# A matmul with bias and residual: the fourth x tile loaded behind W, transposes in the middle of a tile's products, another transfer list

## The chip, the core and the metric

The kernel runs on one core of one Trainium2 chip. The metric is the device time in microseconds (us); smaller is better. The core has five engines that matter here: TensorE (PE in the profile, with its weight loads as PEld), VectorE (DVE), ScalarE (ACT), GpSimd (POOL) and SyncE (SP). SP computes nothing in this kernel. It only issues the transfers between HBM and SBUF. Every transfer is cut over the core's 16 DMA engines, which work in parallel, each in the order of issue.

## The reference

```python
batch, m, k, n = 16, 512, 1024, 768      # all float32
def reference(x, weight, bias, residual):
    return (np.matmul(x, weight) + bias + residual).astype(np.float32)
```

Flattened, x is 8192 x 1024, W is 1024 x 768, and residual and output are 8192 x 768.

## The kernel before, in words

The 8192 rows are worked through as 64 tiles (t = 0 to 63) of 128 rows each, in four groups S of 16 tiles (J = 16). Row number (S, p, j) of x lies in partition p of tile 16 S + j, so that a transfer of several neighbouring tiles moves one long piece for each partition.

SBUF holds a ring X of 16 x tiles in float32, a ring R of 32 rows (one row is a 128 x 768 residual tile, which becomes the output tile in place), a ring XB of four casted tiles, a ring XT of four transposed tiles, and W in bf16 (w_sb). PSUM holds three product tiles PO and two transpose tiles PT. W arrives in four chunks q of 256 rows of K each; its staging place is rows 14 to 21 of R, and it is cast from there into w_sb by operations called wc.

Each tile t takes these steps:

- cast(t): ACT turns the float32 tile X into bf16 XB (in the head VectorE takes some or half of them; "sv" means that ACT and VectorE take a half each).
- transp(t): TensorE transposes the tile in four matrix instructions (two bf16 values are moved as one float32 word) into PT, and VectorE copies PT into XT.
- mm(t, q): for one chunk q of W, two weight loads and four matmuls, two 512 and two 256 columns wide. mm_all(t, range(n_q)) takes all n_q = 4 chunks, so sixteen matmuls a tile.
- finish(t): VectorE adds PSUM and the R row. For t below 14 (EARLY_END), residual has not come yet. There finish writes product plus bias into a spare row of R, and GpSimd adds the residual later. From tile 14 on, GpSimd adds bias to the residual row first, and finish(t) needs that row.
- pool_adds: GpSimd goes through the list ADDS, and stops at the first entry whose residual row or finish isn't there yet in program order.

The order of the work is written out by hand. HEAD_ORDER is the order of the first three tiles' products (HEAD = 3), which run chunk by chunk of W across the tiles, with dummy matmuls (warm) where TensorE would idle. The loop from L352 on takes the tiles 3 to 62, one each: cast of t + 2, GpSimd's adds, transposes of t + 1, all products of t, finish of t - 1. Tile 63 closes the kernel in two pieces of 512 and 256 columns (LAST).

ORDER is the list of transfers, and SP issues them in exactly this order (pump, L174). An entry is (kind, S, first j, end j): 'x' and 'r' load tiles of x and residual, 'w' and 'b' load a chunk of W and the bias, 's' stores output rows, 'c' stores a piece of the last tile. If an entry has to wait, all the entries behind it wait too. An x tile waits for the cast of the tile 16 before it (the ring X), a residual row from tile 32 on waits for the landing of the store of the row 32 before it (the ring R), and a store waits for the finishes or adds of its rows. A wait for a transfer is a wait for all 16 of its DMA engines.

```python
    for t in range(HEAD, n_t):
        cast(t + 2)
        pool_adds(t + 1)
        transp(t + 1)
        if t < n_t - 1:
            mm_all(t, range(n_q))
        finish(t - 1)
        pool_adds(t + 1)
```

Of the kernel before, what the change touches and what calls it, by code (L numbers as in the profile page):

```python
# [19 lines left out]
EARLY_END = 14  # L20
TMP_ROW = 16
W_ROW = 14
ADDS = [10, 14, 3, 2, 4, 15, 11, 1, 5, 13, 7, 6, 12, 9, 0, 8]
HEAD_ORDER = [('cast', 0, 'v'), ('cast', 1, 's'), ('tr', 0), ('tr', 1), ('wc', 0, 0, 's'), ('wc', 0, 1, 'g'),
 ('warm', 3), ('mm', 0, 0), ('mm', 1, 0), ('cast', 2, 'sv'), ('cast', 3, 'sv'), ('warm', 3),
 ('tr', 2), ('tr', 3), ('wc', 1, 0, 's'), ('wc', 1, 1, 'v'), ('mm', 2, 0), ('mm', 0, 1),
 ('mm', 1, 1), ('mm', 2, 1), ('wc', 2, 0, 's'), ('wc', 2, 1, 'v'), ('mm', 0, 2), ('mm', 1, 2),
 ('mm', 2, 2), ('wc', 3, 0, 's'), ('wc', 3, 1, 'v'), ('bias',), ('cast', 4, 'sv'), ('mm', 0, 3),
 ('fin', 0), ('mm', 1, 3), ('mm', 2, 3)]
ORDER = [('x', 0, 0, 2), ('w', 0, 0, 2), ('x', 0, 2, 4), ('w', 1, 0, 2), ('b', 0, 0, 0), ('w', 2, 0, 2),  # L30
 ('w', 3, 0, 2), ('x', 0, 4, 6), ('x', 0, 6, 10), ('r', 0, 0, 6), ('x', 0, 10, 14),
 ('r', 0, 6, 16), ('x', 0, 14, 16), ('x', 1, 0, 6), ('r', 1, 0, 6), ('x', 1, 6, 16),
 ('r', 1, 6, 16), ('s', 0, 0, 16), ('x', 2, 0, 6), ('r', 2, 0, 6), ('x', 2, 6, 16),
 ('r', 2, 6, 16), ('s', 1, 0, 16), ('x', 3, 0, 6), ('r', 3, 0, 7), ('x', 3, 6, 16),
 ('r', 3, 7, 16), ('s', 2, 0, 16), ('s', 3, 0, 10), ('s', 3, 10, 13),
 ('s', 3, 13, 15), ('c', 3, 15, 0), ('c', 3, 15, 1)]
OUTSIDE = 4
LAST = [(0, 512), (512, 256)]

# [78 lines left out]
def kernel(  # L118
# [14 lines left out]
    n_q = K // (2 * P)  # L133
    n_t = M // P
# [29 lines left out]
    def rows(a, b, cs=range(len(chunks))):  # L164
        return [("R", r % RR, c) for r in range(a, b) for c in cs]
# [4 lines left out]
    done = set()  # L170
    queue = list(ORDER)
    stores = []
# [48 lines left out]
    def mark(*what):  # L221
        done.add(what)
        pump()

    def copy(eng, dst, src, rd, wr):
        op(eng, lambda e: (e.copy if eng == "act" else e.tensor_copy)(out=dst, in_=src), rd, wr)  # L226

    def plus(eng, dst, a, b, rd, wr):
        op(eng, lambda e: e.tensor_add(out=dst, in0=a, in1=b), rd, wr)  # L229
# [4 lines left out]
    def cast(t, how="s"):  # L234
        if t < n_t:
            assert ("x", t) in done, t
            src, dst, h = X[:, t % XR, :], XB[t % XB_N], K // 2
            rd, wr = [("X", t % XR)], [("XB", t % XB_N, i) for i in range(2)]
            if how == "sv":
                copy("act", dst[:, 0:h], src[:, 0:h], rd, wr[:1])  # L240
                copy("dve", dst[:, h:K], src[:, h:K], rd, wr[1:])
            else:
                copy("act" if how == "s" else "dve", dst, src, rd, wr)
            mark("cast", t)

    def transp(t):
        if t < n_t:
            words, pt = XB[t % XB_N].bitcast(FP32), PT[t % 2]
            for q in range(n_q):
                op("pe", lambda e, q=q: e.transpose(out=pt[:, q, :], in_=words[:, ts(q, P)], identity=ident),  # L250
                   [("XB", t % XB_N, 2 * q // n_q), "ident"], [("PT", t % 2)])
            copy("dve", XT[t % XT_N].rearrange("p q m e -> p (q m e)"),
                 pt.rearrange("p q m -> p (q m)").bitcast(BF16), [("PT", t % 2)], [("XT", t % XT_N)])
# [11 lines left out]
    def mm(t, q, e, parts, po, wr):  # L265

        lhsT, rd = XT[t % XT_N][:, q, :, e], [("XT", t % XT_N)]
        op("pe", lambda g: g.ldweights(lhsT), rd)  # L268
        for n0, nl, to in parts:
            times(po[:, to:to + nl], lhsT, w_sb[:, q, e, n0:n0 + nl], q == 0 and e == 0, q == n_q - 1 and e == 1,  # L270
                  [*rd, ("w", q, e)], [wr])

    def mm_all(t, qs):
        for q in qs:
            for e in range(2):
                mm(t, q, e, [(n0, nl, n0) for n0, nl in chunks], PO[t % HEAD], ("PO", t % HEAD))

    def row(t, n0=0, nl=N):
        return R[:, t % RR, n0:n0 + nl]

    def tmp(t):
        return R[:, TMP_ROW + t, :]

    adds = list(ADDS) + list(range(max(ADDS) + 1, n_t))

    def pool_adds(upto):
        for t in [t for t in adds if t <= upto]:
            if ("r", t) not in done or (t < EARLY_END and ("fin", t) not in done):
                return
            adds.remove(t)  # L290
            r, rk = row(t), rows(t, t + 1)
            if t < EARLY_END:
                plus("pool", r, r, tmp(t), rk + rows(TMP_ROW + t, TMP_ROW + t + 1), rk)
                mark("add", t)
                mark("out", t)
            else:
                plus("pool", r, r, bias_sb, rk + ["bias"], rk)
                mark("add", t)

    def finish(t):  # L300
        p, pk = PO[t % HEAD], ("PO", t % HEAD)
        if t < EARLY_END:
            plus("dve", tmp(t), p, bias_sb, [pk, "bias"], rows(TMP_ROW + t, TMP_ROW + t + 1))
            mark("fin", t)
        else:
            assert ("add", t) in done, t
            plus("dve", row(t), p, row(t), [pk] + rows(t, t + 1), rows(t, t + 1))
            mark("out", t)
# [18 lines left out]
    for kind, *a in HEAD_ORDER:  # L327
# [10 lines left out]
        elif kind == "wc":  # L338
            q, e, eng = a
            r = W_ROW + 2 * q + e  # L340
# [11 lines left out]
    for t in range(HEAD, n_t):  # L352
        cast(t + 2)
        pool_adds(t + 1)
        transp(t + 1)
        if t < n_t - 1:
            mm_all(t, range(n_q))
        finish(t - 1)
        pool_adds(t + 1)
    t = n_t - 1  # L360
    for i, (n0, nl) in enumerate(LAST):
        b = (t - 2 * i) % HEAD
# [45 lines left out]
```

## Time and profile before

| what | value |
|---|---|
| time, median of 3 runs (lowest, highest) | 210.14 us (210.11, 210.18) |
| span of the profiled execution, first to last instruction | 208.5 us |
| what the median holds beyond that span | 1.6 us |
| TensorE busy | 201.6 us, 97% |
| the transfer queue's share of 16 DMA engines | 97.9% |
| VectorE, ScalarE, GpSimd busy | 105.3, 66.1 and 115.2 us |
| bytes read, written | 61.88 MB, 25.17 MB |
| transfers in the list | 33 |

For the profiled execution itself, the profile gives the span and no separate device time. The span runs on the profile's own clock from the first to the last instruction; the runs' times were taken without it. So the two are compared through the 1.6 us between span and median. The busy shares of two resources are above 97%, TensorE's and the DMA engines', and a share alone doesn't tell which of the two sets the end. That needs the last few microseconds of the trace.

### The profile page before, as it was taken

How to read it: one execution, taken by the hardware profiler on the slowest of the kernel's cores; microseconds unless marked ns; L12 is line 12 of the kernel's file. 1: busy time of each engine (PE TensorE's matmuls, PEld its weight loads, DVE VectorE, ACT ScalarE, POOL GpSimd, SP SyncE). 2: the span in 40 equal slices, each digit the busy share in tenths (PEclk: the TensorE clock that was granted, in tenths of full speed). 3: DMA queues.
4: the chain of work that ended last, by engine and by line, in shares of the span. 5: the costliest groups of instructions: out<-in, count | busy, mean ns of one | idle time of the engine just before them, and what ended most of it. 6: DMA issues, size and time to landing. Idle time of an engine off the chain costs nothing.

```text
span 208.5 us, 2492 instructions
## 1 busy us (share of the span) xinstructions
PE 201.6 (97%) x1298; PEld 80.8 (39%) x794; DVE 105.3 (51%) x141; ACT 66.1 (32%) x69; POOL 115.2 (55%) x71
## 2 busy tenths in 40 slices
PE   7899999999999999999999999999999999999991
PEld 2333434443443444344334434433443443344340
DVE  1457555445545543654554454555445545544542
ACT  2444522402640282420280094230092047430000
POOL 1100029859999904999029801999207960899200
PEclk9999999999999999999999999999999999999998
DMA  5999999899999999999998999999999999999985
GB/s 216 425 425 445 426 423 475 385 427 425 485 409 416 449 395 438 453 396 437 410 493 387 432 445 429 443 443 385 423 450 468 416 398 471 415 443 417 427 351 232
DMA packets 4627, 87.20 MB, mean 418 GB/s; under 512 B 516, under 2 KB 644, under 8 KB 1416
## 3 DMA queue, kind: packets, MB, share of 16 engines
q1 hardware_dynamic: 4616, 87.05, 97.9%
q8 instruction: 8, 0.13, 0.2%
q14 instruction: 3, 0.02, 0.0%
HBM read 61.88 MB, written 25.17 MB: 417 GB/s over the span
## 4 chain that ended last, share of the span: by engine, by line
PE 92%; DMA 4%; DVE 1%; SPq 0%; ACT 0%; issue 0%
PE psum_o L257 79%; PE pt L250 13%; DMA x_tile<-in_x_dram 4%; SPq L168 0%; DVE xt L226 0%; ACT xb L226 0%; DVE ro L229 0%; SPq L403 0%; SPq L371 0%
## 5 line engine op out<-in xcount | busy, mean ns | idle before, releaser
L257 PE MATMUL psum_o<-w_sb,xt 128*128 128x256 bf16 (+1 forms) x1024 | 176.6, 326 | 0.5 <-DVE xt L226 0.5
L229 POOL TENSOR_TENSOR ro<-ro,bias_sb 128x768 f32<-128x768 f32 x50 | 88.8, 1817 | 46.9 <-DMA ro<-in_residual_dram 46.9
L226 ACT CAST xb<-x_tile 128x1024 bf16<-128x1024 f32 (+1 forms) x63 | 61.3, 1023 | 117.1 <-DMA x_tile<-in_x_dram 88.6
L268 PEld LDWEIGHTS <-xt 128*128 128x128 bf16 x520 | 50.9, 98 | 102.9 <-issue 101.0
L226 DVE COPY xt<-pt 128x1024 bf16<-128x1024 bf16 x64 | 44.1, 691 | 83.4 <-PE pt L250 83.4
L229 DVE TENSOR_TENSOR ro<-psum_o,ro 128x768 f32<-128x768 f32 (+2 forms) x51 | 47.6, 934 | 6.5 <-POOL ro L229 4.5
L250 PE MATMUL pt<-ident,xb 128*128 128x128 f32 x256 | 38.3, 274 | 0.6 <-DVE xb L226 0.4
L229 POOL TENSOR_TENSOR ro<-ro 128x768 f32<-128x768 f32 x14 | 24.9, 1818 | 25.0 <-DMA ro<-in_residual_dram 24.9
L250 PEld LDWEIGHTS pt<-ident,xb 128*128 128x128 f32 x256 | 29.7, 141 | 15.6 <-issue 12.3
L229 DVE TENSOR_TENSOR ro<-psum_o,bias_sb 128x768 f32<-128x768 f32 x14 | 13.2, 948 | 0.0
L312 PE MATMUL psum_o<-warm 128*128 128x512 bf16 x18 | 6.3, 506 | 1.4 <-DVE warm_a L232 1.4
L226 DVE CAST xb<-x_tile 128x512 bf16<-128x512 f32 (+1 forms) x4 | 1.9, 492 | 6.2 <-DMA x_tile<-in_x_dram 6.2
L226 ACT CAST w_sb<-ro 128x768 bf16<-128x768 f32 x4 | 3.3, 832 | 3.7 <-DMA ro<-in_weight_dram 3.7
L226 POOL CAST w_sb<-ro 128x768 bf16<-128x768 f32 x1 | 0.8, 822 | 6.0 <-DMA ro<-in_weight_dram 6.0
L312 PEld LDWEIGHTS psum_o<-warm 128*128 128x128 bf16 x18 | 2.1, 124 | 4.5 <-issue 2.7
L226 DVE CAST w_sb<-ro 128x768 bf16<-128x768 f32 x3 | 1.7, 557 | 2.0 <-DMA ro<-in_weight_dram 2.0
L226 ACT ACT_TABLE_LOAD x1 | 1.3, 1283 | 0.9 <-SPq L371 0.9
L329 DVE STREAM_SHUFFLE bias_sb<-bias_row 128x768 f32<-128x768 f32 x1 | 1.0, 1007 | 0.0
L232 DVE MEMSET warm<- 128x256 uint32 x1 | 0.3, 272 | 1.1 <-SPq L371 1.1
L232 DVE MEMSET bias_row<- 128x768 f32 x1 | 0.7, 698 | 0.2 <-issue 0.2
L232 POOL MEMSET ident<- 128x128 f32 x1 | 0.2, 204 | 0.5 <-SPq L371 0.5
L320 POOL TENSOR_SCALAR_AFFINE_SELECT ident<-ident 128x128 f32<-128x128 f32 x1 | 0.3, 292 | 0.2 <-POOL ident L232 0.2
(7 smaller groups left out, 0.7 us busy)
## 6 DMA issues: line engine op xcount, KB each, us to landing
out_dram<-ro SPq DMA_DIRECT2D x3, 6144.0 KB, 34.6
x_tile<-in_x_dram SPq DMA_DIRECT2D x3, 5120.0 KB, 24.5
ro<-in_residual_dram SPq DMA_DIRECT2D x3, 3840.0 KB, 32.4
x_tile<-in_x_dram SPq DMA_DIRECT2D x3, 3072.0 KB, 34.0
ro<-in_residual_dram SPq DMA_DIRECT2D x3, 2304.0 KB, 18.7
x_tile<-in_x_dram SPq DMA_DIRECT2D x4, 1024.0 KB, 10.9
x_tile<-in_x_dram SPq DMA_DIRECT2D x2, 2048.0 KB, 23.4
out_dram<-ro SPq DMA_DIRECT2D x1, 3840.0 KB, 13.3
```

Source lines behind the costliest of these rows:

```text
L226: op(eng, lambda e: (e.copy if eng == "act" else e.tensor_copy)(out=dst, in_=src), rd, wr)
L229: op(eng, lambda e: e.tensor_add(out=dst, in0=a, in1=b), rd, wr)
L232: op(eng, lambda e: e.memset(dst, v), [], [wr])
L250: op("pe", lambda e, q=q: e.transpose(out=pt[:, q, :], in_=words[:, ts(q, P)], identity=ident), [("XB", t % XB_N, 2 * q // n_q), "ident"], ...
L257: return e.add_instruction(mybir.InstMatmult(name=nc.get_next_instruction_name(), ins=[e.lower_ap(rhs), e.lower_ap(lhsT, for_matmul_weight ...
L268: op("pe", lambda g: g.ldweights(lhsT), rd)
L312: op("pe", lambda e: e.matmul(PO[i][:, 0:512], lhsT=warm[:, 0:P], rhs=warm, start=True, stop=True), ["warm"], [("PO", i)])
L320: op("pool", lambda e: e.affine_select(out=ident, in_=ident, compare_op=mybir.AluOpType.not_equal, fill=1.0, base=0, pattern=[[-1, P]], ch ...
L329: op("dve", lambda e: e.stream_shuffle(out=bias_sb, in_=bias_row, mask=[0] * QUAD), ["bias_row"], ["bias"])
```

## The change

Four things are changed, and nothing that is computed:

- ORDER: x tiles 2 and 3 are two transfers now. Tile 2 stays ahead of the second chunk of W, and tile 3 goes behind the fourth. The x, residual and store entries after that are cut elsewhere, and three of the old pieces are spread out: group 2's residuals are loaded in four pieces, its predecessor's store (group 1) in two pieces between them, and the last four residual rows are loaded behind the store of group 2. The list has 39 entries where it had 33.
- HEAD_ORDER: tile 2 is cast, transposed and multiplied alone, the second run of three dummy matmuls is gone, tile 3 is cast after the last chunk of W and transposed between the last products of tiles 1 and 2, and the bias is spread (bias) earlier. The cast of tile 4 goes to ACT alone, at the head's end.
- The loop: the transposes of tile t + 1 stand between the products of chunks 0, 1 and of chunks 2, 3 of tile t, and finish(t - 1) with GpSimd's adds stands ahead of them.
- ADDS: GpSimd takes the first sixteen rows in their natural order.

```diff
--- before.py
+++ after.py
@@ -20,20 +20,19 @@
 EARLY_END = 14
 TMP_ROW = 16
 W_ROW = 14
-ADDS = [10, 14, 3, 2, 4, 15, 11, 1, 5, 13, 7, 6, 12, 9, 0, 8]
+ADDS = [0, 1, 2, 3, 4, 5, 6, 7, 8, 9, 10, 11, 12, 13, 14, 15]
 HEAD_ORDER = [('cast', 0, 'v'), ('cast', 1, 's'), ('tr', 0), ('tr', 1), ('wc', 0, 0, 's'), ('wc', 0, 1, 'g'),
- ('warm', 3), ('mm', 0, 0), ('mm', 1, 0), ('cast', 2, 'sv'), ('cast', 3, 'sv'), ('warm', 3),
- ('tr', 2), ('tr', 3), ('wc', 1, 0, 's'), ('wc', 1, 1, 'v'), ('mm', 2, 0), ('mm', 0, 1),
- ('mm', 1, 1), ('mm', 2, 1), ('wc', 2, 0, 's'), ('wc', 2, 1, 'v'), ('mm', 0, 2), ('mm', 1, 2),
- ('mm', 2, 2), ('wc', 3, 0, 's'), ('wc', 3, 1, 'v'), ('bias',), ('cast', 4, 'sv'), ('mm', 0, 3),
- ('fin', 0), ('mm', 1, 3), ('mm', 2, 3)]
-ORDER = [('x', 0, 0, 2), ('w', 0, 0, 2), ('x', 0, 2, 4), ('w', 1, 0, 2), ('b', 0, 0, 0), ('w', 2, 0, 2),
- ('w', 3, 0, 2), ('x', 0, 4, 6), ('x', 0, 6, 10), ('r', 0, 0, 6), ('x', 0, 10, 14),
- ('r', 0, 6, 16), ('x', 0, 14, 16), ('x', 1, 0, 6), ('r', 1, 0, 6), ('x', 1, 6, 16),
- ('r', 1, 6, 16), ('s', 0, 0, 16), ('x', 2, 0, 6), ('r', 2, 0, 6), ('x', 2, 6, 16),
- ('r', 2, 6, 16), ('s', 1, 0, 16), ('x', 3, 0, 6), ('r', 3, 0, 7), ('x', 3, 6, 16),
- ('r', 3, 7, 16), ('s', 2, 0, 16), ('s', 3, 0, 10), ('s', 3, 10, 13),
- ('s', 3, 13, 15), ('c', 3, 15, 0), ('c', 3, 15, 1)]
+ ('warm', 3), ('mm', 0, 0), ('mm', 1, 0), ('cast', 2, 'sv'), ('tr', 2), ('mm', 2, 0), ('wc', 1, 0, 's'),
+ ('wc', 1, 1, 'v'), ('mm', 0, 1), ('mm', 1, 1), ('mm', 2, 1), ('bias',), ('wc', 2, 0, 's'),
+ ('wc', 2, 1, 'v'), ('mm', 0, 2), ('mm', 1, 2), ('mm', 2, 2), ('wc', 3, 0, 's'), ('wc', 3, 1, 'v'),
+ ('cast', 3, 'sv'), ('mm', 0, 3), ('fin', 0), ('mm', 1, 3), ('tr', 3), ('mm', 2, 3), ('cast', 4, 's')]
+ORDER = [('x', 0, 0, 2), ('w', 0, 0, 2), ('x', 0, 2, 3), ('w', 1, 0, 2), ('b', 0, 0, 0), ('w', 2, 0, 2),
+ ('w', 3, 0, 2), ('x', 0, 3, 4), ('x', 0, 4, 6), ('x', 0, 6, 9), ('r', 0, 0, 7), ('x', 0, 9, 13),
+ ('r', 0, 7, 16), ('x', 0, 13, 16), ('x', 1, 0, 7), ('r', 1, 0, 7), ('x', 1, 7, 16), ('r', 1, 7, 16),
+ ('s', 0, 0, 16), ('x', 2, 0, 7), ('r', 2, 0, 2), ('r', 2, 2, 9), ('x', 2, 7, 16), ('r', 2, 9, 12),
+ ('s', 1, 0, 8), ('r', 2, 12, 16), ('s', 1, 8, 16), ('x', 3, 0, 6), ('r', 3, 0, 6), ('x', 3, 6, 16),
+ ('r', 3, 6, 12), ('s', 2, 0, 16), ('r', 3, 12, 16), ('s', 3, 0, 4), ('s', 3, 4, 11), ('s', 3, 11, 14),
+ ('s', 3, 14, 15), ('c', 3, 15, 0), ('c', 3, 15, 1)]
 OUTSIDE = 4
 LAST = [(0, 512), (512, 256)]
 
@@ -352,11 +351,13 @@
     for t in range(HEAD, n_t):
         cast(t + 2)
         pool_adds(t + 1)
+        if t < n_t - 1:
+            mm_all(t, range(n_q // 2))
+        finish(t - 1)
+        pool_adds(t + 1)
         transp(t + 1)
         if t < n_t - 1:
-            mm_all(t, range(n_q))
-        finish(t - 1)
-        pool_adds(t + 1)
+            mm_all(t, range(n_q // 2, n_q))
     t = n_t - 1
     for i, (n0, nl) in enumerate(LAST):
         b = (t - 2 * i) % HEAD
```

## Prediction

> **What bounds the kernel now.** I read the page first (shares and slices), then the chain of waits, then the last microseconds. From the page:
>
> ```profile
> PE 201.6 (97%) x1298; PEld 80.8 (39%) x794; DVE 105.3 (51%) x141; ACT 66.1 (32%) x69; POOL 115.2 (55%) x71
> ...
> DMA  5999999899999999999998999999999999999985
> ...
> q1 hardware_dynamic: 4616, 87.05, 97.9%
> ```
>
> Two candidates: TensorE and the transfers are both above 97%. The chain of waits names TensorE:
>
> ```profile
> by line: PE psum_o L257 79.4%; PE pt L250 13.0%; DMA x_tile<-in_x_dram 3.9%; SPq L168 0.4%; DVE xt L226 0.3%; ACT xb L226 0.3%; issue 0.3%; DVE ro L229 0.2%; SPq L403 0.0%; SPq L371 0.0%
> ...
> 12.22 6.74 PE psum_o L257 x40
> 19.00 0.66 PE pt L250 x4
> ...
> 22.38 0.44 PE pt L250 x4
> 22.81 2.60 PE psum_o L257 x16
> ```
>
> From 12.2 us on TensorE has no gap: a tile costs 0.44 for four transposes and 2.60 for sixteen products, 3.04. But this view goes back from the last store to the engine that released it. It doesn't ask whether that store then stood behind others. VectorE's timeline and a table of the last stages do:
>
> ```profile
> 201.65 0.96 DVE L229 TENSOR_TENSOR ro<-psum_o,ro 128x768 f32<-128x768 f32 x1 [1.11 <-PE psum_o L257]
> 203.30 0.69 DVE L229 TENSOR_TENSOR ro<-psum_o,ro 128x512 f32<-128x512 f32 x1 [0.70 <-PE psum_o L257]
> 204.18 0.42 DVE L229 TENSOR_TENSOR ro<-psum_o,ro 128x256 f32<-128x256 f32 x1 [0.18 <-PE psum_o L257]
> ```
>
> ```profile
> 200.00:201.00 1.00, 1.00 (x8) 0.32 (x4) 0.53 (x1) 0.00 (x0) 0.00 (x0) 1.00 0.73 307
> ...
> 202.00:203.00 1.00, 1.00 (x6) 0.49 (x5) 0.60 (x1) 0.00 (x0) 0.00 (x0) 1.00 0.68 286
> 203.00:204.00 1.00, 1.00 (x10) 0.69 (x7) 0.69 (x1) 0.00 (x0) 0.00 (x0) 1.00 0.74 310
> 204.00:205.00 1.00, 0.14 (x2) 0.00 (x0) 0.42 (x1) 0.00 (x0) 0.00 (x0) 1.00 1.03 418
> ```
>
> The last two columns are the DMA engines' share and GB/s. Some engines are idle from 200 to 204, and it looks as if stores were missing. The landing marks of the single DMA engines say otherwise. Rows 48 to 57 land between 199.41 (first engine) and 201.69 (last), rows 58 to 60 between 202.13 and 204.44, rows 61 and 62 between 205.73 and 206.28, the two last pieces at 206.93 and 207.27 at the latest. The last engine took 2.75, 1.84, 0.65 and 0.34 us for its 73.7, 49.2, 16.4 and 8.2 KB, which is 24 to 27 GB/s: it has no gap to the end. Following the last landings backwards I find none at all back to the first transfer (14.52 us for the store of 81.00 to 95.52, 12.14 for the x load of 157.66 to 169.80, 27 GB/s each). So the late DMA engine sets the end, and the fast ones idle for it. TensorE ties with it: released at 202.61, the store of rows 61 and 62 landed on the fast engines only 0.55 us before the late one.
>
> **The head: a gain on TensorE.** An x tile is 32.8 KB an engine. Packets in the trace take 309 ns for 8192 bytes and 1815 for 49152, so 27.2 GB/s and 8 ns for each packet: a tile takes 1.20 us. With tile 3 behind W, chunk 1 lands at 11.96 - 1.20 = 10.76, chunk 2 at 12.70, chunk 3 at 14.57, tile 3 at 15.85, tiles 4 and 5 at 18.3 as before. Tile 2 lands at 8.88; cast 0.62, transposes from 9.8 on (after the products that ended at 9.79), copy 0.69, product of chunk 0 at 11.1, where before it began at 12.22. Then nine (tile, chunk) units of 0.65: chunk 2 is wanted at 13.7 (cast 13.6), chunk 3 at 15.7 (cast 15.4). The second three dummies fall out of a stretch in which TensorE waited anyway. Tile 3 is transposed at 17.0, the first three tiles end near 18.0, tile 3's products at 21.15 with tile 4's transposes in them. Before, the same work was done at 22.21: gain 1.06. Two moved steps cost nothing here: the bias spread (1.01 on VectorE, its row landed by 11.0) fits between the cast of chunk 1 (to 11.7) and chunk 2's landing at 12.70, and would push chunk 2's cast by what it is late; tile 4's cast, 1.04 on ACT alone, ends at 19.3, and its transposes are wanted at 19.4. Bounds: a gain of 0.8 (ACT and VectorE each 0.1 to 0.2 late at one chunk) to 1.1.
>
> **The transposes in mid-tile.** The same instructions, so no busy time. What moves is cover: the copy XT (0.69) of the next tile has 1.30 us of products after the transposes, where it had 2.60. It stands behind finish(t - 1) (0.95) on VectorE, which starts with the tile. So if finish waits for GpSimd over 1.30 + 0.44 + 1.30 - 0.95 - 0.69 = 1.4 us, TensorE stalls.
>
> **x and residual cut elsewhere.** x 6 to 8 lands at 18.25 + 3.69 = 21.94. Residual 0 to 6 (7 rows of 0.90, 6.40 with packets) would follow at 28.34. One engine lost 1.32 us in this place before: residual 0 to 5 landed at 28.14 to 28.64 on 15 engines and at 29.96 on the last, after a 16 KB instruction packet at 23.84. I keep that: 29.66. x 9 to 12 lands at 34.55, cast ends at 35.7:
>
> ```profile
> 30.03 10.67 POOL L229 TENSOR_TENSOR ro<-ro 128x768 f32<-128x768 f32 x6 [21.57 <-DMA ro<-in_residual_dram]
> ...
> 34.93 3.89 ACT L226 CAST xb<-x_tile 128x1024 bf16<-128x1024 f32 x4 [7.81 <-DMA x_tile<-in_x_dram]
> ```
>
> The lower line is where tile 10 came at almost the same time, wanted at 37.4. Now tile 9 comes there, wanted at 22.45 + 4 x 3.04 = 34.6: stall 1.1 us (0.4 if the late engine were only 0.6 late), and the head's gain is spent. The other batches keep a margin after that (tile 32: cast by 105.1, wanted at 105.6).
>
> **ADDS in natural order.** Residual 7 to 15 lands at 42.8; nine adds of 1.78 (six in 10.67) put row 14 seven places back, done at 57.0. Product 14 ends at 55.7. So finish(14) waits 1.3, just under the 1.4 that the copy allows, and row 16 (landed near 61.5, added by 63.3, wanted at 61.8) waits 1.5: 0 to 0.3 us of stall, I take 0.15. TensorE ends 0.2 later than before, net: -1.06 + 1.1 + 0.15.
>
> **Six more transfers.** One more x entry, three more residual, two more stores. Each is eight more packets an engine: 8 x 8 ns, and a semaphore packet of 9 ns: 0.075 us. Landings agree: loads of 65.5 and 327.7 KB an engine take 2.48 and 12.14, of which the bytes explain all but 0.07 to 0.1. The late engine has no gap to hide it in: 6 x 0.076 = 0.46 us. Lower bound by the last small stores (0.04 each): 0.24. No place of the new list lets SP run dry: the longest wait, residual 32 for the landing of group 0's store near 95, has 8.5 us of x behind that store in the queue.
>
> The Trainium skill speaks against small transfers: DMA: Bandwidth & Descriptors, section "Bandwidth", wants 1 MiB and more for each, and its "Anatomy" section gives each a fixed cost of about 2.0 us. By that, six would add 12 us and the time would be about 222; as the landings show 0.07 to 0.1 in a full queue, I take this as latency that a queue hides.
>
> The same skill's TensorE: Matmul & The Clock Gate, Part 1, has the clock halved after an idle window of about 3.4 us. The new stall is 1.1 us, the trace of before shows no idle time of that length after 6.5 us and a mean clock of 0.996, so no run here shows it yet; if the stall did halve the clock for one window, some 1.7 us more would be spent.
>
> **The end.** The last full store is one row instead of two, so TensorE's side lies 1.2 us ahead of the late engine: finish(62) ends near 202.8, transfers began to move some 1.3 us after their release in this place before (202.61, first landing 205.73, less 1.84), and the row's turn in the late queue is near 205.3. So 0.2 us later on TensorE costs nothing, and the transfers' 0.46 all arrives: span 208.5 + 0.46 = 209.0, and with the same 1.6 us around it 210.14 + 0.46 = 210.60. A measurement can tell about 0.2%, 0.42 us, from no change: the forecast is just above it.
>
> **The rivals.**
> - The transfers' fixed cost is half: 210.4, no difference. For it: the small stores at the end. Against: packets and loads. 0.19.
> - Faster: the lateness of the last engine (2.3 us behind the first) comes from instruction packets, and another list may shift which engine they hit. If it shrinks by over 0.9 us, the saving beats the 0.46; TensorE's side then stops it at 0.7 below the time before: 209.4 to 209.7. Against: the packets come about every 24 us with TensorE's program, which keeps its length. 0.09.
> - Slower by more: TensorE binds, as the stall at tile 9 and GpSimd's waits add up to twice what I found, against 1.06 gained. TensorE's side lies 1.2 ahead of the late engine's new end, and 0.2 of the net loss is in that already; so the point is a net loss of 1.4 (stalls of 2.5), and beyond it each 0.1 is paid: with stalls of 3.0, 210.60 + 0.5 = 211.1. Rows 14 and 16 lie near the edge. 0.12.
> - The forecast, 210.4 to 210.8: 0.60, two thirds of it above the 0.2%.
>
> Slower 0.40 + 0.12 = 0.52, same 0.20 + 0.19 = 0.39, faster 0.09. The range 210.1 to 211.2 leaves out the faster rival and the far end of the slower one.
>
> **What would show it.** Right: TensorE's products of tile 0 to 2 end near 18.0; one wait of the transposes for ACT of about 1.1 near 34.6; GpSimd waits on VectorE of 1.3 and 1.5 near 57 and 63; last landings 0.3 to 0.5 later than 207.27, and the last engine without a gap. Wrong: a stretch where SP waits and the DMA share falls below 0.9 in mid-span; a late engine that is not 2 us late; TensorE's last product after 205; a clock below 0.99.

## The result, and the profile after

The changed kernel takes 210.72 us (median of 8 runs, 210.66 to 210.83), beside 210.16 us for the kernel before (8 runs, 209.92 to 210.39). The ratio is 1.0026 with a 95% interval of 1.0016 to 1.0037, so it is slower by 0.56 us, or 0.26%. The span of the profiled execution goes from 208.5 to 208.9 us; the profiled run itself took 210.69 us.

The page of the changed kernel, the lines that answer to those of before:

```profile
PE 200.0 (96%) x1270; PEld 81.0 (39%) x791; DVE 110.2 (53%) x140; ACT 67.1 (32%) x69; POOL 115.4 (55%) x71
...
q1 hardware_dynamic: 5480, 87.05, 97.9%
```

The queue moves the same 87.05 MB in 5480 packets instead of 4616. Those are six more transfers of 8 payload packets and a semaphore packet on each of the 16 engines: 6 x 16 x 9 = 864. Its share is still 97.9%, so the longer list filled more time and not less. The chain of waits names TensorE in 79% of the span (67.6 and 11.6) and a load of x in 13.5%:

```profile
by line: PE psum_o L256 67.6%; DMA x_tile<-in_x_dram 13.5%; PE pt L249 11.6%; SPq L167 2.5%; issue 1.2%; DVE ro L228 0.9%; ACT xb L225 0.5%; DVE xt L225 0.3%; SPq L404 0.0%; DVEq L103 0.0%; ACTq L103 0.0%; SPq L372 0.0%
```

TensorE's timeline shows where that load comes in, and a second place where TensorE stands. The bracket at the end is the idle time ahead of the group, and its releaser. It counts from the modelled end of the group before; sixteen products follow each other in 2.60 us, and by that the two places cost 1.14 us (34.78 to 35.92) and 0.48 us (58.97 to 59.45):

```profile
32.17 2.76 PE L256 MATMUL psum_o<-w_sb,xt 128*128 128x512 bf16 x16
35.92 0.66 PE L249 MATMUL pt<-ident,xb 128*128 128x128 f32 x4 [0.99 <-ACT xb L225]
...
57.67 1.46 PE L256 MATMUL psum_o<-w_sb,xt 128*128 128x512 bf16 x8
59.45 1.48 PE L256 MATMUL psum_o<-w_sb,xt 128*128 128x512 bf16 x8 [0.31 <-DVE xt L225]
```

The first is tile 9: its x landed at 34.75. The second is the copy XT of tile 16, late behind finish(14). VectorE's timeline has that, the head, and the end:

```profile
16.44 0.96 DVE L228 TENSOR_TENSOR ro<-psum_o,bias_sb 128x768 f32<-128x768 f32 x1 [0.17 <-PE psum_o L256]
17.53 0.69 DVE L225 COPY xt<-pt 128x1024 bf16<-128x1024 bf16 x1
...
57.84 0.96 DVE L228 TENSOR_TENSOR ro<-psum_o,ro 128x768 f32<-128x768 f32 x1 [2.31 <-PE pt L249]
58.71 0.68 DVE L225 COPY xt<-pt 128x1024 bf16<-128x1024 bf16 x1
...
63.60 0.96 DVE L228 TENSOR_TENSOR ro<-psum_o,ro 128x768 f32<-128x768 f32 x1 [1.51 <-POOL ro L228]
...
204.55 1.02 DVE L228 TENSOR_TENSOR ro<-psum_o,ro 128x512 f32<-128x512 f32 x2 [1.21 <-PE psum_o L256]
```

The last piece is added by 205.57, where before it was 204.60. The table of the last stages (the columns are as before: granted clock, the five engines, clock, DMA share, GB/s):

```profile
204.00:205.00 1.00, 0.95 (x9) 0.60 (x7) 0.45 (x1) 0.00 (x0) 0.00 (x0) 1.00 0.89 356
205.00:206.00 1.00, 0.00 (x0) 0.00 (x0) 0.57 (x2) 0.00 (x0) 0.00 (x0) 1.00 0.39 156
206.00:207.00 1.00, 0.00 (x0) 0.00 (x0) 0.00 (x0) 0.00 (x0) 0.00 (x0) 1.00 0.89 327
```

The 0.39 from 205 to 206 is a hole that the kernel before did not have (0.93 there). The landing marks say more: each DMA engine marks the landing of its share of a transfer, so a transfer of rows has 16 marks, and the last one counts. Row 62 landed on the last engine at 206.33, the two last pieces at 207.31 and 207.66. Their bytes need 0.65 and 0.34 us on the late engine (these were the steps of before), so the first should have landed at 206.98 and was held up 0.33 us by VectorE.

Against before, the last landing moves by 207.66 - 207.27 = 0.39 us. In the landing marks of these two executions it is made up like this. The first x landed 0.31 earlier (5.43 for 5.74), but that was lost again at x tile 2, which landed 1.59 us after W's first chunk where its bytes and packets need 1.28. Tiles 4 and 5 landed at 18.30, before at 18.25, so 0.05 later. From there to the last landing of the last full store it took 188.0 us in both kernels. The last pieces took 1.33 us for 0.99, so 0.34 more, and that comes from compute's end. So in this execution the longer list costs 0.05 us by its last full store. The packets of its five further transfers are there (0.37 by the prediction's price). But at three loads of groups 0 and 1 the late engine lost 1.70 us beyond bytes and packets, where it had lost 1.84, and its other steps are 0.24 shorter in sum, none by more than 0.1. Whether the runs' 0.56 is made in the same way is what the experiments ask.

In the eleven profiles of the table below that have a time of their own and keep the products, the time is 3.03 to 3.05 us more than the last landing. By that the profiled execution of before was one of 210.30, 0.14 above its median, and a changed kernel whose compute ends as in this profile comes to at least some 207.66 + 3.03 = 210.69.

### The profile page after: what moved, and what is told of

Its sections match the earlier page's. It is cut to its first block, busy times and chain, and to the rows that moved or that the text cites. A ratio compares the mean times of both kernels' runs of the same rounds, so it can differ in the third digit from the quotient of the medians.

```text
span 208.9 us, 2514 instructions
## 1 busy us (share of the span) xinstructions
PE 200.0 (96%) x1270; PEld 81.0 (39%) x791; DVE 110.2 (53%) x140; ACT 67.1 (32%) x69; POOL 115.4 (55%) x71
## 3 DMA queue, kind: packets, MB, share of 16 engines
q1 hardware_dynamic: 5480, 87.05, 97.9%
## 4 chain that ended last, share of the span: by engine, by line
PE 79%; DMA 13%; SPq 2%; DVE 1%; issue 1%; ACT 1%; DVEq 0%; ACTq 0%
PE psum_o L256 68%; DMA x_tile<-in_x_dram 13%; PE pt L249 12%; SPq L167 2%; DVE ro L228 1%; ACT xb L225 1%; DVE xt L225 0%; SPq L404 0%; DVEq L103 0%; ACTq L103 0%; SPq L372 0%
## 5 line engine op out<-in xcount | busy, mean ns | idle before, releaser
L256 PE MATMUL psum_o<-w_sb,xt 128*128 128x256 bf16 (+1 forms) x999 | 173.8, 324 | 2.5 <-DVE xt L225 1.1
L225 ACT CAST xb<-x_tile 128x1024 bf16<-128x1024 f32 (+1 forms) x63 | 62.3, 1030 | 117.7 <-DMA x_tile<-in_x_dram 78.3
L249 PEld LDWEIGHTS pt<-ident,xb 128*128 128x128 f32 x256 | 30.2, 142 | 15.9 <-issue 12.5
```

The costliest lines, as they stand in the source:

```text
L256: return e.add_instruction(mybir.InstMatmult(name=nc.get_next_instruction_name(), ins=[e.lower_ap(rhs), e.lower_ap(lhsT, for_matmul_weight ...
```

## The experiments

Three theories stand against each other. **A:** the late DMA engine sets the end in both kernels, and the longer list makes it later. **B:** TensorE sets the end already in the kernel before. **C:** in the changed kernel it is TensorE's side that sets the end, as the hole at 205 suggests. Every kernel was timed beside the kernel before (median 210.13 to 210.17), and the ratio is to that; "last add" and "last landing" are of its profile, and "lateness" is how far the last of the 16 engines lies behind the first at the store of rows 48 to 57 (in the changed list 52 to 58).

| kernel | median us | ratio to before, 95% interval | last add | last landing | lateness |
|---|---|---|---|---|---|
| before | 210.16 | | 204.60 | 207.27 | 2.28 |
| after | 210.72 | 1.0026 (1.0016 to 1.0037) | 205.57 | 207.66 | 2.22 |
| before_less | 210.06 | 0.9999 (0.9990 to 1.0008) | 203.38 | 207.13 | 2.20 |
| after_less | 210.84 | 1.0032 (1.0022 to 1.0043) | 204.44 | 207.32 | 1.81 |
| after_narrow | 211.02 | 1.0040 (1.0026 to 1.0053) | 204.61 | 207.99 | 2.54 |
| after_t9 | 210.80 | 1.0028 (1.0017 to 1.0038) | 205.16 | 207.76 | 2.33 |
| after_adds | 211.01 | 1.0047 (1.0034 to 1.0059) | 205.18 | 207.92 | 2.53 |
| before_mid | 211.82 | 1.0081 (1.0068 to 1.0094) | 206.10 | 208.79 | 2.11 |
| head_mid | 211.42 | 1.0063 (1.0051 to 1.0075) | 206.14 | 208.40 | 1.97 |
| before_cuts | 210.80 | 1.0025 (1.0013 to 1.0036) | 204.55 | 207.62 | 1.88 |
| before_noprod | 210.42 | 1.0017 (1.0002 to 1.0031) | 196.08 | 207.11 | 2.18 |
| after_noprod | 211.77 | 1.0080 (1.0057 to 1.0102) | 204.41 | 208.08 | 2.86 |
| hybrid | 210.04 | 0.9992 (0.9984 to 1.0001) | 204.51 | 207.01 | 1.91 |
| hybrid_between | 210.72 | 1.0026 (1.0016 to 1.0035) | 204.45 | 207.66 | 2.41 |

**Less work for TensorE.** The same two lines go into either kernel, into mm_all:

```diff
+            if t == 57 and 0 < q < 3:
+                continue
```

> The kernel before, with the products of chunks 1 and 2 of tile 57 left out (its output rows are then not the reference's): TensorE has 1.3 us less to do, late in the span, and no transfer changes. Theory A (the forecast): the late DMA engine sets the end of the kernel before, so the time stays, 0 to 0.2 us lower than the kernel before in the same rounds. Theory B (the chain of waits taken at its word: TensorE sets the end): 1.3 us lower, near 208.9.

VectorE's timeline of before_less (last add), and its table of the last stages:

```profile
202.96 0.42 DVE L229 TENSOR_TENSOR ro<-psum_o,ro 128x256 f32<-128x256 f32 x1 [0.18 <-PE psum_o L257]
```

```profile
203.00:204.00 1.00, 0.00 (x0) 0.00 (x0) 0.39 (x1) 0.00 (x0) 0.00 (x0) 1.00 0.98 402
204.00:205.00 1.00, 0.00 (x0) 0.00 (x0) 0.00 (x0) 0.00 (x0) 0.00 (x0) 0.99 1.00 405
205.00:206.00 1.00, 0.00 (x0) 0.00 (x0) 0.00 (x0) 0.00 (x0) 0.00 (x0) 0.50 0.68 257
```

All compute is over at 203.38, 1.22 us earlier than before, and the time is the same. The DMA engines work on without a hole until the first of them are through. B falls: in the kernel before, at least 1.2 us of TensorE's busy end is free.

> The changed kernel with the same products of tile 57 left out. Theory A (the forecast's sum: six more transfers on a late DMA engine without a gap make the whole difference): no change against the changed kernel, 0.5 above the kernel before. Theory C (from the trace after: the transfers alone would have ended at 206.33 + 0.65 + 0.34 = 207.32 instead of 207.66, the rest is TensorE's and VectorE's later end): 0.3 to 0.4 lower than the changed kernel, so 0.1 to 0.3 above the kernel before. Theory B: 1.3 lower than the changed kernel.

After_less was not lower than the changed kernel (210.84 for 210.72). Its profiled execution happened to be its fastest run (210.35) and alone would have spoken for C. The other six runs (210.66 to 211.20) don't. In the next kernel the number of instructions stays the same (the products of tile 57 become 64 columns wide):

```diff
-                mm(t, q, e, [(n0, nl, n0) for n0, nl in chunks], PO[t % HEAD], ("PO", t % HEAD))
+                mm(t, q, e, [(n0, 64 if t == 57 else nl, n0) for n0, nl in chunks], PO[t % HEAD], ("PO", t % HEAD))
```

> The changed kernel with the sixteen products of tile 57 only 64 columns wide (its output row is then not the reference's): as many instructions as before, so the instruction packets stay where they are, but TensorE ends 2.1 us earlier. Theory A (the list of transfers makes the whole difference): no change against the changed kernel, 0.5 to 0.6 above the kernel before. Theory C (TensorE's later end, made by the mid-tile place and the arrival of x 9 to 12, holds the last stores back): 0.3 to 0.4 lower than the changed kernel, 0.2 to 0.3 above the kernel before, and the last three landings follow each other by the bytes alone (0.98, 0.65, 0.34 us).

VectorE's timeline and the last stages of after_narrow:

```profile
203.59 1.02 DVE L228 TENSOR_TENSOR ro<-psum_o,ro 128x512 f32<-128x512 f32 x2 [1.22 <-PE psum_o L256]
```

```profile
205.00:206.00 1.00, 0.00 (x0) 0.00 (x0) 0.00 (x0) 0.00 (x0) 0.00 (x0) 1.00 0.92 354
206.00:207.00 1.00, 0.00 (x0) 0.00 (x0) 0.00 (x0) 0.00 (x0) 0.00 (x0) 0.96 0.65 241
```

TensorE was to end 2.1 us earlier here. It ended 0.97 earlier, less than in after_less (1.12), since the narrow products give the copy XT of tile 58 too little cover and TensorE waits for it at 186. The last add is 0.96 us earlier than in the changed kernel and the hole at 205 is gone (0.92 for 0.39), yet the time is 211.02. The last engine goes from 207.01 to 207.65 and 207.99, 0.64 and 0.34 for the two pieces, which is their bytes. So C's forecast fails: a microsecond taken off TensorE's end brings no time back, and in these kernels the changed list alone comes to 210.8 to 211.0.

What sets the end in the changed kernel itself is left open by this. In its profile it was compute, by 0.33 us. Its eight runs lie within 0.17 us of each other, around the 210.69 that this end gives, while the runs of the four relieved kernels (after_less, after_narrow, after_t9, after_adds) spread over 0.5 to 0.85 us and have higher medians. From tiles 4 and 5 to the last full store three of their profiles take 188.4 to 188.5 us, and that of after_less 188.0, as the changed kernel's does. So two things can each make about the measured 0.56: compute's later end, and a delay in the list that some executions have and others don't. The one execution recorded with neither is the profile of after_less, at 210.35.

**The wait at tile 9.** Tile 9 is cast from tile 8's place, so it no longer waits for its own load (its values are then tile 8's):

```diff
-            src, dst, h = X[:, t % XR, :], XB[t % XB_N], K // 2
+            at = 8 if t == 9 else t % XR
+            src, dst, h = X[:, at, :], XB[t % XB_N], K // 2
```

> The changed kernel with the cast of tile 9 reading tile 8's place in SBUF (its output row is then not the reference's), so that it no longer waits for the landing of x 9 to 12. The wait of 1.1 us at tile 9 should be gone. If TensorE were held up there by that one transfer, its end would come 1.1 us earlier. By the arrival times it is held up by supply: the next new batch, x 13 to 15, lands near 46.6 and is wanted near 46.9, less 1.1 for the cast, so a wait of 0.8 appears there, and TensorE ends only 0.2 to 0.3 earlier; time 0.1 to 0.3 lower than the changed kernel by theory C, the same by theory A.

TensorE's timeline of after_t9, the first group with idle time ahead of it behind the head:

```profile
47.63 0.66 PE L250 MATMUL pt<-ident,xb 128*128 128x128 f32 x4 [0.40 <-ACT xb L225]
```

The wait at 35 is gone and one at tile 13 takes its place, since x tiles come no faster than before. Of the 1.1 us only 0.4 reaches the last add, and none of it the time (210.80).

**GpSimd's list.** The changed kernel with ADDS as before:

```diff
-ADDS = [0, 1, 2, 3, 4, 5, 6, 7, 8, 9, 10, 11, 12, 13, 14, 15]
+ADDS = [10, 14, 3, 2, 4, 15, 11, 1, 5, 13, 7, 6, 12, 9, 0, 8]
```

> The changed kernel with the list ADDS of the kernel before, so GpSimd takes rows 14 and 15 ahead of four others and TensorE's stall of 0.48 us at tile 16 should be gone. Theory A: no change against the changed kernel. Theory C: TensorE's end is 0.48 earlier, of which 0.3 to 0.4 shows before the transfers stop it: as low as the changed kernel without tile 57's products.

The last add comes 0.4 us earlier, and the time is higher, not lower: 211.01. The natural order costs TensorE a little, and with the old one no time comes back. The last engine's extra time here lies at one load, of residual rows 12 to 15 of group 2, which took 0.44 us more than its bytes and packets. More of that below ("Which of the transfers?").

**The loop alone, and the loop with the head.** The transposes are put in mid-tile in the kernel before, with its list, head and ADDS:

```diff
     for t in range(HEAD, n_t):
         cast(t + 2)
         pool_adds(t + 1)
-        transp(t + 1)
         if t < n_t - 1:
-            mm_all(t, range(n_q))
+            mm_all(t, range(n_q // 2))
         finish(t - 1)
         pool_adds(t + 1)
+        transp(t + 1)
+        if t < n_t - 1:
+            mm_all(t, range(n_q // 2, n_q))
```

> The kernel before with the changed loop alone: transposes of the next tile in mid-tile, the list, the head and ADDS as before. Theory A: the transfers set the end, so no change as long as TensorE's side is less than 0.5 us later. But here the head's gain is missing while finish has only 1.4 us of cover: I work out a stall of about 1.0 us at tile 3, and 0.4 near tile 24, less the 0.4 of transposes that the head no longer waits for, so TensorE ends about 0.8 later and its last store is released near 205.4: 0.2 to 0.5 higher than the kernel before. Theory that the mid-tile place is free of charge: no change.

Head_mid adds HEAD_ORDER of the changed kernel, and x tiles 2 and 3 as two transfers with tile 3 behind W.

> The kernel before with the changed loop and the changed head, tile 3 behind W (34 transfers, one more), the rest of the list and ADDS as before. Theory A: one more transfer, 0.05 to 0.08, if TensorE's side is not over 0.5 us later; but row 16 comes to finish 1.6 us too late for the shorter cover, and TensorE ends about 0.8 later than before in spite of the head's gain: 0.3 to 0.5 higher. If the six transfers are the whole price of the change and TensorE's waits cost nothing: 0.05 to 0.1 higher.

Before_mid, with TensorE's and VectorE's timelines and the last stages:

```profile
84.44 1.48 PE L257 MATMUL psum_o<-w_sb,xt 128*128 128x512 bf16 x7 [0.75 <-DVE xt L226]
```

```profile
63.68 0.96 DVE L229 TENSOR_TENSOR ro<-psum_o,ro 128x768 f32<-128x768 f32 x1 [1.98 <-POOL ro L229]
64.55 0.68 DVE L226 COPY xt<-pt 128x1024 bf16<-128x1024 bf16 x1
```

```profile
203.00:204.00 1.00, 1.00 (x7) 0.43 (x5) 0.47 (x1) 0.00 (x0) 0.00 (x0) 1.00 0.18 74
204.00:205.00 1.00, 1.00 (x8) 0.61 (x7) 0.68 (x2) 0.00 (x0) 0.00 (x0) 1.00 0.04 8
```

Here is what a kernel looks like in which TensorE's side does set the end: the DMA engines stand for more than a microsecond (0.18, 0.04) while TensorE works. Finish waits for a residual row ahead of 63.68, and the copy XT stands behind it. That costs TensorE little there (0.15), but the same ahead of 84.44 costs it 0.9 us, and with 0.6 at tile 3 the last add comes 1.5 later. The time is 1.7 us longer (0.0081 x 210.13), where I expected 0.2 to 0.5. Head_mid's head doesn't buy it back: it has stalls of 1.3 and 0.8 us near 65 and 84. So the transposes in mid-tile are the one part of the change that can cost over a microsecond. The changed kernel's list and ADDS hold that loss to 0.5.

**More transfers of the same bytes.** The kernel before, with its long x, residual and store pieces cut in two or three: 45 entries for 33. An excerpt:

```diff
- ('x', 1, 6, 16), ('r', 1, 6, 16), ('s', 0, 0, 16),
+ ('x', 1, 6, 11), ('x', 1, 11, 16), ('r', 1, 6, 11), ('r', 1, 11, 16), ('s', 0, 0, 5), ('s', 0, 5, 10), ('s', 0, 10, 16),
```

> The kernel before with twelve more transfers and nothing else: long x, residual and store pieces of groups 1 to 3 are cut in two or three, in the same order. Theory A with the forecast's price of 0.076 us each: 0.9 higher than the kernel before. With the price that the landings of the trace after give (0.06): 0.7 higher. Theory B, or a queue that hides the packets: 0 to 0.2 higher.

The page's queue line:

```profile
q1 hardware_dynamic: 6344, 87.05, 98.2%
```

Twelve more transfers cost 0.0025 x 210.2 = 0.53 us by the ratio and 0.64 to 0.67 by the medians, so 0.044 to 0.056 us each (0.02 to 0.06 by the interval of the ratio). The price of 0.076 was too high by 0.02 to 0.03. By this, six would cost 0.26 to 0.34.

**No products at all.** The products of tiles 3 to 62 are left out of either kernel (the loop runs without mm_all).

> The kernel before without the products of tiles 3 to 62 (their output rows are then not the reference's), all transfers, casts, transposes and adds kept. TensorE has some 150 us less to do and its program is much shorter, so that most of the 16 KB instruction packets should be gone. Theory A with the late engine made by instruction packets: the last engine's lateness falls from 2.2 us to at most 1.5 and the time by 0.5 to 1.8 us, to 208.3 to 209.6. If the lateness has another cause: no change, 210.1.

> The changed kernel without the same products. With TensorE out of the way, what is left between this and the kernel before without products is the list of transfers alone. Theory A with the forecast's 0.076 us for each of the six more: 0.46 above it; with the price of the run with twelve more cuts (0.05 each): 0.3 above it. Theory C (TensorE's later end makes a part of the 0.56 that was measured): the rest of the 0.56 is gone here. If the difference stays 0.5 to 0.6, the list does it all.

From the page of before, and then of before_noprod, the line of the instruction queue:

```profile
q8 instruction: 8, 0.13, 0.2%
```

```profile
PE 80.3 (39%) x336; PEld 48.6 (23%) x314; DVE 103.6 (50%) x141; ACT 64.6 (31%) x69; POOL 114.7 (55%) x71
...
q8 instruction: 2, 0.03, 0.1%
```

TensorE's program is shorter and fetches two 16 KB packets instead of eight. The first comes at 38.5 us for 23.8. With it moves the step that makes one engine late: residual 0 to 5 lands last at 28.70 for 29.96, and the 1.3 us are lost at the next residual load instead. In after_noprod the first packet comes at 52.0, and the load that loses 1.4 us is the one under way then, x 0 to 6 of group 1. Three places of the packet, three places of the loss: the packet is the cause of the late engine. But the time of before_noprod is no lower, though its last add is 8.5 us earlier, and the lateness at the end is nearly the same (2.18): one packet on one engine is enough, and six fewer save nothing. Some of what was saved came back at the second residual load of group 1, where the late engine lost 0.55 us here and 0.35 in before. I had expected 0.5 to 1.8 us less; that was wrong.

After_noprod is 1.35 us above before_noprod, far over the 0.3 to 0.46 expected; its six runs spread from 210.96 to 212.84. Compute doesn't hold up the end here (the last two pieces land 0.65 and 0.33 us after the store and piece ahead of them, which is their bytes), so the list alone can lose more than its packets. Its last engine lost 0.56 us at the same load as in after_adds.

**Which of the transfers?** The hybrid takes only what the change does to the head (HEAD_ORDER, x tile 3 behind W, mid-tile transposes for tiles 3 to 7), and leaves the rest of the list, the loop and ADDS as before: 34 entries.

```diff
+MID = 7
...
-        transp(t + 1)
+        if t > MID:
+            transp(t + 1)
         if t < n_t - 1:
-            mm_all(t, range(n_q))
+            mm_all(t, range(n_q // 2 if t <= MID else n_q))
         finish(t - 1)
         pool_adds(t + 1)
+        if t <= MID:
+            transp(t + 1)
+            mm_all(t, range(n_q // 2, n_q))
```

> The version that the runs point to: head as changed with tile 3 behind W, transposes in mid-tile for tiles 3 to 7 alone and ahead of the tile's products from tile 8 on, the rest of the list and ADDS as before; 34 transfers. TensorE should keep the head's gain and end 0.8 to 0.9 earlier than before, the last piece finished near 203.8 instead of 204.60. Theory A: the transfers set the end, one more costs 0.05, so 0 to 0.1 above the kernel before although TensorE is nearly a microsecond ahead. Theory B (TensorE sets the end): 0.8 lower, near 209.3.

It is the fastest version, at 210.04, but not separable from the kernel before (the interval reaches 1.0001). Its last add was to come 0.8 us earlier and came 0.09 earlier (204.51), as TensorE kept little of the head's gain (0.63 us at tile 5), so this run doesn't tell A from B a second time. Hybrid_between is the hybrid with three more entries, those of the changed list that put a load between stores:

```diff
- ('r', 2, 6, 16), ('s', 1, 0, 16),
+ ('r', 2, 6, 12), ('s', 1, 0, 8), ('r', 2, 12, 16), ('s', 1, 8, 16),
...
- ('r', 3, 7, 16), ('s', 2, 0, 16),
+ ('r', 3, 7, 12), ('s', 2, 0, 16), ('r', 3, 12, 16),
```

> The hybrid's list with three more transfers only: residual 6 to 16 of group 2 in two pieces, the store of group 1 in two halves with the second residual piece between them, and residual 7 to 16 of group 3 in two pieces with the store of group 2 between them, all as the changed list has them. The rest, TensorE's order, the head and GpSimd's list, is the hybrid's. Theory A1 (a further transfer costs its packets, wherever it stands: 0.044 to 0.067 us each in the runs so far): +0.13 to +0.2 over the hybrid's 210.04, so 210.2; every landing step of the last engine fits its bytes within 0.1 us. Theory A2 (a load that stands between two stores makes the late engine later by 0.4 to 0.6 us, as in most profiles with the changed list): +0.5 to +0.8, so 210.6 to 210.8, and the landing step of that load is 0.4 to 0.6 us above its bytes.

VectorE's last add in the hybrid, and then in hybrid_between:

```profile
204.09 0.42 DVE L223 TENSOR_TENSOR ro<-psum_o,ro 128x256 f32<-128x256 f32 x1 [0.18 <-PE psum_o L251]
```

```profile
204.03 0.42 DVE L223 TENSOR_TENSOR ro<-psum_o,ro 128x256 f32<-128x256 f32 x1 [0.18 <-PE psum_o L251]
```

Compute ends at the same time, and the three transfers cost 0.68 us: 210.72 for 210.04 (by the ratios 0.71; the kernel before stood at 210.16 and 210.17 beside them, and no run of the one reaches into the range of the other, 209.90 to 210.30 and 210.39 to 210.95). At 0.05 each they would have cost 0.15, so A1 falls and A2 holds. In the landing marks the last engine took 4.23 us for the load of residual 12 to 15 of group 3 behind the store of group 2; the same load took 3.61 in the changed kernel's profile, and its bytes and packets need 3.68. That is 0.55 too much, and all the other steps fit their bytes and packets within 0.06 us, but for the first residual load with the instruction packet (1.39). The other load, between the halves of the store of group 1, lost nothing in this execution (3.72), but 0.44, 0.40, 0.56 and 0.61 in after_adds, after_narrow, after_noprod and after_t9. In the changed kernel's own profile neither load lost anything, and in after_less 0.12. So in five of seven profiles such a load cost 0.4 to 0.6 us. That the place beside the store is what does it is the reading that fits; why it does so in some executions only is open.

The packets of these loads show it from the other side. A packet of 12288 bytes takes 0.46 us as a rule. Of the 128 packets of residual 12 to 15 of group 2, which start while other engines still store, 12 took 0.57 to 1.0 us in after_adds and 12 took 0.56 to 0.98 in after_narrow, 10 in after_t9 up to 1.17, 9 in after_less up to 0.79, but only 2 in the profile of the changed kernel. Of the load that cost hybrid_between its 0.55, six took 0.62 to 1.42. A loss shows where they fall on the late engine; the trace doesn't name the engine of a packet, so this is argued and not shown.

## Why the prediction was right, and where its steps were not

**The bound.** That the late DMA engine sets the end, with TensorE close behind, was right for the kernel before (before_less, before_noprod), and for the changed list where TensorE is relieved (after_less, after_narrow, after_t9). In the changed kernel's own profile compute set the end, by 0.33 us. The instruction packet as the source of the lateness was right as well (before_noprod).

**The transfers' term.** The sum, 0.46 us for 0.56 measured, was near, and that was luck. I gave each of the six the same price. The runs show about 0.05 us for a transfer that is only cut (before_cuts), so 0.3 for six, and 0.68 for the three that bring loads beside stores (hybrid_between). In the changed kernel's own profile the six cost 0.05 together, and the late end of compute, which the sum has at nothing, 0.34. A price too high by half and two steps that I didn't have, the place of a load beside a store and the end of compute, made up for each other. The full list and hybrid_between have the same median, 210.72; as compute ends 1.1 us later in the one, that doesn't tell what the two other entries cost.

The prediction also reads the last engine of the kernel before as without a gap back to the first transfer. Besides the 1.3 us that it names, two loads there took 0.19 and 0.34 us more than their bytes and packets (x 0 to 5 and residual 6 to 15 of group 1), and in the changed kernel's profile the loads at these places lost 0.05 and 0.20. So this part differs by a few tenths from one execution to the next, as much as the term itself.

The Trainium skill's price, about 2 us fixed for each DMA (DMA: Bandwidth & Descriptors, the section "Anatomy of one DMA", which gives it for transfers that GpSimd issues, a condition that the prediction left out), would have given 24 us for before_cuts, as an estimate. Measured were 0.53 to 0.67 us, with SP issuing. Where the queue ran empty, the two last pieces of the changed kernel landed 2.1 us after their adds ended (205.24 to 207.31 and 205.57 to 207.66); 0.65 and 0.34 of that are their bytes. That leaves 1.4 to 1.75 us, a little under the page's figure, paid there and not in a full queue.

**The head.** Products of tiles 0 to 2 were to end near 18.0, and did at 17.98. The gain by tile 5's transposes is 0.88 us, not 1.06, but within the bounds of 0.8 to 1.1. What I left out is the cover of one copy: the transposes of tile 3 end at 17.49, its copy XT runs from 17.53 to 18.22, and only one unit of products, to 17.98, stands beside it. So TensorE waits some 0.3 us for it. (Finish(0) ended at 17.40 and didn't delay it.)

**Tile 9.** The wait came where it was put, 1.1 us near 34.6. It lasted 1.14, from 34.78 to 35.92. The granted clock stayed at 1.00 throughout, so the price for a halved clock that the prediction set beside the sum was not paid:

```profile
35.00:36.00 1.00, 0.08 (x1) 0.08 (x2) 0.00 (x0) 1.00 (x2) 1.00 (x2) 1.00 1.03 442
```

**GpSimd at 57 and 63.** The waits of finish came at both places (2.31 us idle ahead of 57.84, 1.51 ahead of 63.60). The second cost nothing, as it should. Finish(14) came 1.9 us after its product (55.94) and not 1.3, which is 0.5 over the cover of the copy, and TensorE lost 0.48 where I took 0.15. GpSimd's timeline has the reason:

```profile
43.10 10.66 POOL L228 TENSOR_TENSOR ro<-ro 128x768 f32<-128x768 f32 x6 [0.73 <-DMA ro<-in_residual_dram]
54.14 1.81 POOL L228 TENSOR_TENSOR ro<-ro 128x768 f32<-128x768 f32 x1 [0.38 <-DVE ro L228]
```

It started 0.3 later than 42.8, and in the natural order the add of row 13 had to wait 0.38 for finish(13), which had only just been done. I counted the places in the list ahead of row 14, not what they wait for. Net, TensorE is 0.8 us later at the end and not 0.2: 0.18 of the difference is the head's, 0.33 this stall's, 0.04 tile 9's.

**The margin at the end.** This step failed in the profiled execution. I put TensorE's side 1.2 us ahead of the late engine; it was 0.33 behind. I took that margin at the last full store, and row 62 was indeed in time; it was the two pieces behind it that were late, and I had not worked out theirs. The first of the last pieces left VectorE some 1.2 us later than before, not 0.2: 0.8 is TensorE's, and 0.4 lies on VectorE. The changed kernel's chain of waits, its last pieces (start, duration, what):

```profile
201.05 3.04 PE psum_o L256 x16
204.09 0.03 issue
204.12 0.02 DVEq L103
204.14 0.41 issue
204.55 1.02 DVE ro L228 x2
```

Ahead of finish(63) VectorE carries out a wait as an instruction by itself (204.12; L103 emits the waits), and the add starts 0.41 later, with nothing in the profile that it waits for. In the kernel before the add started 0.04 after its last product. Why the program has this wait here I did not settle; after_less, after_narrow, after_t9 and after_adds have it too, with 0.41 to 0.43. The rest is the late engine, which was 0.4 earlier than worked out: the list cost 0.05 by row 62 and not 0.46. Ending TensorE up to 1.1 us earlier (after_less) brings no time back: in three of the four profiles with TensorE relieved the list loses about as much. But the margin is used up, and the rival in which TensorE binds was nearer than its 0.12 says: before_mid is that rival, at 211.82, mostly by the cover of the copy that I named for such a stall.

**The faster rival** did not come: with the changed list the lateness went from 1.81 to 2.86 us, with the old one (or the hybrid's) from 1.88 to 2.28.

## What to carry to other kernels

When two resources are above 97%, take 1 to 2 us of work from one of them, in a kernel that leaves it out: the time tells which one sets the end, where the chain of waits may name the other. If the time stays, look whether both ends had come close, as here after the change. In a full queue of long transfers count about 0.05 us for each further one, and look at where it stands: a load put between or behind stores cost 0.4 to 0.6 us here in five of seven profiles. Judge such a list by several runs, as the delay comes in some executions and not in others.

## What the runs showed of the hardware

- One 16 KB instruction packet of TensorE's program makes one DMA engine 1.2 to 1.5 us late (the step of the load under way, in 14 profiles), for the rest of the span, and as each wait is for all 16 engines, the kernel ends with that one (before: lateness 1.8 us after the first residual load, 2.3 at the end).
- Packets of a residual load beside a store can take up to three times as long (12288 bytes: 0.46 us as a rule, 0.6 to 1.4 for two to twelve of 128). The place in the queue isn't all: in the kernel before, 16 packets of 30720 bytes between 75 and 80 us, in a residual load ahead of the first store, took 1.1 to 1.5 times as long as the others, and its late engine lost 0.35 us there. What the cause is in the memory or the engines, no run here shows.
- Taking away TensorE's products altogether doesn't make the transfers faster: before_noprod has 210.42 us and a lateness of 2.18.
- The granted clock fell to 0.50 after the last product, at no fixed distance: in before_less that product ended at 202.92, and the table above has 0.99 for 204 to 205 and 0.50 from 205 on, so about 2.1 us; in the other profiles with products it came 2.6 us (before) to 5.4 us (after_t9) after it.
